# FFN output projection of a hybrid block: all 22 row tiles per span of 512, 256, 256 tokens instead of six groups of row tiles

## The chip, the cores and the metric

The kernel runs on one core of one Trainium2 chip. The metric is the device time of the program in microseconds (us); three executions of the kernel before took 2463.94, 2464.05 and 2467.35 us, and their median is what the changed kernel is compared with. In this text PE is the matrix engine (PEld its weight load), DVE the vector engine, ACT the scalar engine, POOL the GpSimd engine, SP the engine that issues nearly all DMAs (its rows are marked SPq; ACTq is ACT's own DMA queue).

## The reference

One layer of a streaming encoder: a mixer sub-layer (sparse attention beside a Mamba-2 mixer) and a SwiGLU sub-layer, both with a norm before and after. Only the end of the second one is touched:

```python
    h2 = rmsnorm(x, pre_norm_ffn) * (1.0 + scale_f) + shift_f
    u_gate, u_up = jnp.split(h2 @ w_ffn_in, 2, axis=-1)
    f = (jax.nn.silu(u_gate) * u_up) @ w_ffn_out
    x = x + gate_f * rmsnorm(f, post_norm_ffn)
```

There are 1024 tokens, `D_MODEL` is 1024 and `D_FF` 2816, all in float32. The matrix `a = silu(u_gate) * u_up` has 22 row tiles of 128 features (`FT` = 22); f has 8 row tiles of 128.

## The kernel before

Everything is held transposed: features on the 128 partitions, tokens along the row. Each float32 operand of a matmul is split into a high part (rounded to the matmul's `float32r`) and a low part (the rest), and each product is three matmuls: high x high, high x low, low x high. The high part is made by an ACT copy, the low part by a subtraction on DVE or POOL (`split_to`). Weights of one tile of f are read in pieces of up to four 128x128 blocks (256 KB).

`gate_up(t)` makes row tile t of `a` for both halves of 512 tokens and writes it to DRAM (`d_a`); the writes are `d_a<-g` (half 1) and `d_a<-p` or `d_a<-g` (half 0) on SP. The last call (t = 21) runs into the stage that is changed.

The FFN output projection then goes over six groups of 4, 4, 4, 4, 3 and 3 row tiles of `a` (`FFN_GROUPS`). For a group, both halves of `a` are read (`al`, nine buffers of the pool EV) and split (`ah`, `al`); for each of the 8 tiles of f the group's weights come through the stream `W` (four raw buffers, three for the high and three for the low part), and 12 (or 9) matmuls per half make a partial sum in PSUM (`pfo`). The first group's sums are copied to SBUF (`facc`) by ACT, those of the next four are added to it by DVE (line 1398).

The last group is different. Its weights are split beforehand into `foh`, `fol`, and it goes over three spans of tokens, `LAST` = 512, 256 and 256. For a span and each t, `sums` runs 9 matmuls (`pfl`), adds them to `facc` (DVE, line 1414), squares (ACT, line 1416) and sums the squares (DVE `sqm`, line 1418). `rstd` is the norm: matmuls of the squares with ones (line 260), one DVE operation (263) and a power on POOL (265). `rspread` spreads it with PE transposes (`prn`, line 271). `outputs` multiplies `facc` by the gate `gf` and the norm (DVE, 1429), adds the residual `x1l` (read on SP; added by POOL, in the last span by DVE for every second tile, line 1430) and writes `out`. The norm and outputs of a span are written between the sums of the next (after its tiles 2 and 4).

A list scheduler sets the order of each engine's instructions; in the last group PE keeps the order of the code (`in_order`). Each engine and each DMA queue runs its instructions strictly in that order, and a buffer is used again when its last reader is done.

Of the kernel before, what the change touches and what calls it, by code (L numbers as in the profile page):

```python
# [67 lines left out]
def build(tc, a, dbg=None, stop=99, slots=None):  # L68
    nc = tc.nc
    V, S, G, T, SP = nc.vector, nc.scalar, nc.gpsimd, nc.tensor, nc.sync  # L70
    ctx = ExitStack()
# [147 lines left out]
    def dense(outs, pcs, xs):  # L219


        for pi, ((hi, lo), k0, ks) in enumerate(pcs):
            for o, b, sl in outs:
                for i, k in enumerate(ks):
                    for wt, xi in ((hi, 0), (hi, 1), (lo, 0)):
                        T.matmul(o, wt[:, k0 + i, :], xs[k][xi][b][:, sl],  # L226
                                 start=pi == 0 and i == 0 and wt is hi and xi == 0,
                                 stop=pi == len(pcs) - 1 and i == len(ks) - 1 and wt is lo)
# [12 lines left out]
    def wpieces(ks, n=4):  # L241

        return [(W.next(), 0, ks[i:i + n]) for i in range(0, len(ks), n)]

    def split_to(src, hi, lo, lo_eng=None):
        S.activation(hi, src, AF.Copy)
        (lo_eng or V).tensor_tensor(lo, src, f(hi), op=OP.subtract)
# [20 lines left out]
    def rspread(r, nt=4):  # L268
        pt = bank("prn")
        for t in range(nt):  # L270
            T.transpose(pt[:, t * P:(t + 1) * P], r[:, t:t + 1].to_broadcast([P, P]), ident)
        return pt
# [1097 lines left out]
    for t in range(FT):  # L1370
        gate_up(t)

    facc = [R(f"facc{t}") for t in range(8)]
    f0 = 0
    NG = len(FFN_GROUPS)
    for gi, gn in enumerate(FFN_GROUPS):
        AH = [([None, None], [None, None]) for _ in range(gn)]
        for t in range(gn):
            for b in BS:
                r = EV("al")  # L1380
                SP.dma_start(r, d_a[f0 + t][:, half(b)])
                AH[t][0][b], AH[t][1][b] = split(Q if gi % 2 else H_, r, "a")
        ks = list(range(gn))

        def ffn_out(t):
            W.plan([(a["w_ffn_out"][t][:, f0:f0 + gn], gn)])
            return wpieces(ks)

        if gi < NG - 1:
            for t in range(8):  # L1390
                p = [bank("pfo") for b in BS]
                dense([(p[b], b, ALL) for b in BS], ffn_out(t), AH)
                for b in BS:
                    fv = facc[t][:, half(b)]
                    if gi == 0:
                        S.activation(fv, p[b], AF.Copy)
                    else:
                        V.tensor_tensor(fv, fv, p[b], op=OP.add)  # L1398
        else:
            fo = []  # L1400
            for t in range(8):
                raw = W.tile(0, F32)
                SP.dma_start(raw[:, :gn], a["w_ffn_out"][t][:, f0:f0 + gn])
                hi, lo = H_("foh", (P, gn, P), F32R), H_("fol", (P, gn, P), F32R)
                split_to(raw[:, :gn], hi, lo, lo_eng=G)
                fo.append((hi, lo))
            def sums(b, c0, cn):

                sacc = None
                for t in range(8):  # L1410
                    p = bank("pfl")[:, 0:cn]
                    dense([(p, b, slice(c0, c0 + cn))], [(fo[t], 0, ks)], AH)
                    fv = facc[t][:, 512 * b + c0:512 * b + c0 + cn]
                    V.tensor_tensor(fv, fv, p, op=OP.add)
                    sq = EV("sqm")[:, 0:cn]
                    S.activation(sq, fv, AF.Square)
                    if t:
                        V.tensor_tensor(sq, sq, sacc, op=OP.add)
                    sacc = sq
                    yield sacc  # L1420

            def outputs(b, c0, cn, r, end):
                cl = slice(512 * b + c0, 512 * b + c0 + cn)
                prf = rspread(r, cn // P)[:, 0:cn]
                for t in range(8):
# [3 lines left out]
                    V.scalar_tensor_tensor(fv, fv, gf[:, t:t + 1], prf, op0=OP.mult, op1=OP.mult)
                    (V if t % 2 and end else G).tensor_tensor(xr, xr, fv, op=OP.add)  # L1430
                    (S if t % 2 and end else SP).dma_start(a["out"][t][:, cl], xr)

            before = None
            with in_order(mybir.EngineType.PE):
                for span in LAST:
                    for t, sacc in enumerate(sums(*span)):
                        if before and t == 2:
                            before[3] = rstd([before[3]], D, nt=before[2] // P)
                        if before and t == 4:
                            outputs(*before, False)  # L1440
                    before = [*span, sacc]
                before[3] = rstd([sacc], D, nt=before[2] // P)
                outputs(*before, True)
        f0 += gn
# [76 lines left out]
```

## Time and profile before

| what | value |
|---|---|
| device time, three executions | 2463.94, 2464.05, 2467.35 us (median 2464.05) |
| the profiled execution, first to last instruction | 2459.8 us, mean granted clock of PE 0.988 |
| busy share: PE, PEld, DVE, ACT, POOL | 97%, 79%, 61%, 48%, 42% |
| changed stage, first matmul of `pfo` to the end | 2191.97 to 2459.8 us |
| DMA over the span | 341 MB, mean 139 GB/s |

A span is counted inside the program, from the first instruction to the last, so a device time is some 4 us more. Times in a timeline are microseconds from the start of the span. In a row of the timeline stand start, duration, engine, line, operation, output<-inputs, shape and count; what stands in brackets is the idle time before and who ended it. Matmuls overlap: one of 512 columns shows 0.39 us, but the next starts earlier, so its cost is the distance of two starts. In a row of groups, the numbers behind the bar are total busy us and mean ns of one, then the idle time before.

### The profile page before, as it was taken

What the parts mean: (1) busy time and instruction counts of PE and PEld (TensorE: products, weight loads), DVE (VectorE), ACT (ScalarE), POOL (GpSimd) and SP (SyncE); (2) the same over time, 40 slices, a digit from 0 to 9 for tenths busy, and PEclk for the clock granted to TensorE, in tenths of its full rate; (3) what the DMA queues carried; (4) which work ended last, traced back from release to release, by engine and by line L of the source; (5) the groups of instructions that cost most, each with busy time, mean ns of one, the idle gap of its engine ahead of it and who ended that gap; (6) DMA issues with size and microseconds to landing.
All of it is one profiled execution on the core that took longest, in us unless ns stands there. A gap on an engine that the chain in (4) does not pass through costs nothing. (4 is left out here: it accounts for less than half of the span.)

```text
span 2459.8 us, 34881 instructions
## 1 busy us (share of the span) xinstructions
PE 2383.1 (97%) x11946; PEld 1931.1 (79%) x11946; DVE 1496.3 (61%) x3050; ACT 1183.7 (48%) x2285; POOL 1022.3 (42%) x829
## 2 busy tenths in 40 slices
PE   7999999999999999999999999999999999999996
PEld 5788888888788887777776767888777888888886
DVE  4566775698745556765558666455476666552336
ACT  4446665567445545556566565544454222352211
POOL 2722112222234334553336335656676555432233
PEclk9999999999999999999999999999999999999998
DMA  7224122523212222223768775654465444253132
GB/s 268 99 77 130 65 73 78 155 87 103 86 67 92 102 99 91 93 84 123 223 215 260 228 246 172 231 186 161 168 208 171 160 145 163 99 190 113 48 99 90
DMA packets 212834, 341.25 MB, mean 139 GB/s; under 512 B 21249, under 2 KB 85425, under 8 KB 212657
## 3 DMA queue, kind: packets, MB, share of 16 engines
q1 hardware_dynamic: 211936, 338.45, 41.6%
q8 instruction: 94, 1.54, 0.3%
q14 instruction: 84, 0.68, 0.1%
q10 hardware_dynamic: 720, 0.58, 0.1%
HBM read 254.77 MB, written 87.32 MB: 139 GB/s over the span
## 5 line engine op out<-in xcount | busy, mean ns | idle before, releaser
L152 POOL TENSOR_TENSOR wlo<-wraw,whi 128x512 fp32r<-128x512 f32 (+1 forms) x282 | 380.7, 1351 | 769.4 <-ACT whi L151 698.5
L151 ACT ACTIVATE whi<-wraw 128x512 fp32r<-128x512 f32 (+1 forms) x282 | 175.4, 623 | 319.0 <-PE pfo L226 110.5
L1283 PE MATMUL p<-xh,wr 128*128 128x512 f32 x880 | 274.4, 391 | 3.8 <-DVE g L1333 3.6
L1283 PEld LDWEIGHTS p<-xh,wr 128*128 128x128 f32 x880 | 165.8, 188 | 39.1 <-DVE g L1333 4.0
L1277 POOL TENSOR_TENSOR wr<-a,wr 128x512 fp32r<-128x512 f32 x110 | 152.7, 1402 | 103.6 <-ACT wr L1276 70.6
L1283 PE MATMUL p<-xl,wr 128*128 128x512 f32 x440 | 171.8, 391 | 0.0
L778 ACT ACTIVATE lg<-lg,mx 128x256 f32<-128x256 f32 (+7 forms) x128 | 98.2, 769 | 74.7 <-DVE mx L775 73.5
L1276 ACT ACTIVATE wr<-a 128x512 fp32r<-128x512 f32 x110 | 67.7, 628 | 123.1 <-PE p L1283 98.0
L226 PE MATMUL pfo<-ah,wlo 128*128 128x512 f32 x304 | 118.1, 389 | 0.0
L226 PE MATMUL pfo<-al,whi 128*128 128x512 f32 x304 | 117.9, 389 | 0.0
L226 PE MATMUL pfo<-ah,whi 128*128 128x512 f32 x304 | 117.8, 389 | 0.0
L317 POOL TENSOR_TENSOR adaw<-adaw,cs 128x512 f32<-128x512 f32 x64 | 66.7, 1044 | 114.7 <-DMA adaw<-ada_w 109.4
L1398 DVE TENSOR_TENSOR facc<-facc,pfo 128x512 f32<-128x512 f32 x64 | 43.9, 686 | 112.0 <-PE pfo L226 112.0
L1283 PE MATMUL p<-h2h,wr 128*128 128x512 f32 x352 | 111.1, 393 | 0.0
L638 ACT ACTIVATE junk<-acc,cand__2203 128x1024 bf16<-128x1024 f32 (+2 forms) x96 | 86.2, 898 | 45.5 <-DVE cand__2203 L681 28.0
L226 PE MATMUL pos<-yw,whi 128*128 128x512 f32 x256 | 101.7, 397 | 3.6 <-DVE yw L1126 3.6
L226 PE MATMUL pos<-yh,whi 128*128 128x512 f32 x256 | 101.4, 396 | 1.7 <-ACT yh L1125 1.7
L226 PE MATMUL pos<-yh,wlo 128*128 128x512 f32 x256 | 101.5, 397 | 1.1 <-POOL wlo L152 1.1
L589 DVE SCALAR_TENSOR_TENSOR acc<-rel,widx,acc 128x384 f32<-128x384 f32 (+2 forms) x90 | 87.0, 986 | 24.9 <-ACT rel L584 24.7
L584 ACT ACTIVATE rel<-prel 128x512 f32<-128x512 f32 (+3 forms) x160 | 77.3, 524 | 48.4 <-PE prel L583 44.8
L1283 PEld LDWEIGHTS p<-xl,wr 128*128 128x128 f32 x440 | 83.0, 189 | 17.4
L799 PE MATMUL pt<-ident,lg 128*128 128x128 f32 x576 | 87.4, 277 | 7.1 <-ACT lg L778 6.6
(573 smaller groups left out, 6978.2 us busy)
## 6 DMA issues: line engine op xcount, KB each, us to landing
wraw<-w_in SPq DMA_DIRECT2D x130, 256.0 KB, 2.6
a<-w_ffn_in SPq DMA_DIRECT2D x124, 256.0 KB, 3.0
adaw<-ada_w SPq DMA_DIRECT2D x64, 256.0 KB, 2.7
al<-d_ac SPq DMA_DIRECT2D x32, 512.0 KB, 5.8
wraw<-w_o_ssd SPq DMA_DIRECT2D x64, 256.0 KB, 3.2
al<-d_a SPq DMA_DIRECT2D x44, 256.0 KB, 5.3
d_a<-g SPq DMA_DIRECT2D x40, 256.0 KB, 2.5
ada<-ada_p SPq DMA_DIRECT2D x16, 512.0 KB, 6.5
```

Of the source, the lines that this page charges most:

```text
L151: behind(S.activation(hi[:, :kt], raw[:, :kt], AF.Copy))
L152: behind(G.tensor_tensor(lo[:, :kt], raw[:, :kt], f(hi[:, :kt]), op=OP.subtract))
L226: T.matmul(o, wt[:, k0 + i, :], xs[k][xi][b][:, sl], start=pi == 0 and i == 0 and wt is hi and xi == 0, stop=pi == len(pcs) - 1 and i == l ...
L317: behind(G.tensor_tensor(t, t, cs[:, 4 * h:4 * h + 4, None].to_broadcast([P, 4, P]), op=OP.mult))
L584: S.activation(rel[:, 512 * b:512 * b + w_], pr[:, 0:w_], AF.Relu)
L589: V.scalar_tensor_tensor(acc[i][:, 0:n], rel[:, 0:n], ws, acc[i][:, 0:n], op0=OP.mult, op1=OP.add)
L638: S.activation(jk, y, AF.Sign, scale=-1.0, bias=a_, accum_out=o)
L778: S.activation(lg[:, 0:n], lg[:, 0:n], AF.Exp, scale=-1.0, bias=m, accum_out=mx[:, 3:4])
L799: T.transpose(ptv[:, hh, t, :], PR[hh, t][:, j * P:(j + 1) * P], ident)
L1276: S.activation(w[:, 0], src, AF.Copy)
L1277: G.tensor_tensor(w[:, 1], src, f(w[:, 0]), op=OP.subtract)
L1283: T.matmul(p, w[:, wi, i], X[x][i][xi], start=start and i == 0 and k == 0, stop=i == 3 and k == 2, skip_group_check=True)
```

## The change

The six groups and `facc` go. For each span of `LAST` all 22 row tiles of `a` are read and split at once (`a_load`), and for each tile t of f a single sum of 66 matmuls runs in one PSUM bank, with six weight pieces (`ffn_w`: k = 0-3, 4-7, ..., 20-21). The weights are read and split anew in each span: 48 pieces per span, 144 in all, where there were 48 loads. In the spans of 256 the low part of every second piece is made by DVE, otherwise by POOL. Four raw buffers remain; the high and low parts have five places. ACT squares the sum straight from PSUM and copies it, scaled with `gf`, to `fv`; `outputs` then multiplies by the norm only. The next span's `a` is loaded after tile 3 of the present span, a span's norm stands after tile 1 and its outputs after tile 2 of the next.

```diff
-    facc = [R(f"facc{t}") for t in range(8)]
-    for gi, gn in enumerate(FFN_GROUPS):
...
-        if gi < NG - 1:
-            for t in range(8):
-                p = [bank("pfo") for b in BS]
-                dense([(p[b], b, ALL) for b in BS], ffn_out(t), AH)
-                for b in BS:
-                    fv = facc[t][:, half(b)]
-                    if gi == 0:
-                        S.activation(fv, p[b], AF.Copy)
-                    else:
-                        V.tensor_tensor(fv, fv, p[b], op=OP.add)
...
-                    dense([(p, b, slice(c0, c0 + cn))], [(fo[t], 0, ks)], AH)
-                    fv = facc[t][:, 512 * b + c0:512 * b + c0 + cn]
-                    V.tensor_tensor(fv, fv, p, op=OP.add)
-                    sq = EV("sqm")[:, 0:cn]
-                    S.activation(sq, fv, AF.Square)
...
-                    xr = Q("x1l")[:, 0:cn]
-                    SP.dma_start(xr, d_x1[t][:, cl])
-                    fv = facc[t][:, cl]
-                    V.scalar_tensor_tensor(fv, fv, gf[:, t:t + 1], prf, op0=OP.mult, op1=OP.mult)
...
+    def a_load(s, b, c0, cn):
+        xs = []
+        for k in range(FT):
+            raw = EV("al")[:, 0:cn]
+            SP.dma_start(raw, d_a[k][:, 512 * b + c0:512 * b + c0 + cn])
+            hi, lo = a_tile(s, k, cn)
+            split_to(raw, hi, lo)
+            xs.append((hi, lo))
+        return xs
...
+    slots_hi = [("w1", n_slots["hi"])] * 3 + [("adaw", 2)] * 2
+    slots_lo = [("w2", n_slots["lo"])] * 3 + [("uh", 1), ("ul", 1)]
+    def ffn_w(t, k0, n, share):
+        i = len(pieces)
+        raw = w_tile(0, "fw")[:, 0:n]
...
+        SP.dma_start(raw, a["w_ffn_out"][t][:, k0:k0 + n])
+        split_to(raw, hi, lo, lo_eng=V if share and i % 2 else G)
...
+    def sums(s, b, c0, cn, fv):
+        xs, sacc = XS[s], None
+        for t in range(8):
+            p = bank("pfo")[:, 0:cn]
+            for k0 in range(0, FT, 4):
+                n = min(4, FT - k0)
+                w = ffn_w(t, k0, n, s > 0)
+                for k in range(k0, k0 + n):
+                    for i, (wi, xi) in enumerate(P3):
+                        T.matmul(p, w[wi][:, k - k0], xs[k][xi], start=k == 0 and i == 0, stop=k == FT - 1 and i == 2)
+            sq = EV("sqm")[:, 0:cn]
+            S.activation(sq, p, AF.Square)
+            S.activation(fv[t], p, AF.Copy, scale=gf[:, t:t + 1])
+            if t:
+                V.tensor_tensor(sq, sq, sacc, op=OP.add)
+            sacc = sq
+            yield sacc
...
+            xr = EV("x1l")[:, 0:cn]
+            SP.dma_start(xr, d_x1[t][:, cl])
+            V.tensor_tensor(fv[t], fv[t], prf, op=OP.mult)
+            (V if t % 2 and end else G).tensor_tensor(xr, xr, fv[t], op=OP.add)
+            (S if t % 2 and end else SP).dma_start(a["out"][t][:, cl], xr)
...
+        for s, (b, c0, cn) in enumerate(LAST):
+            fv = f_tiles(s, cn)
+            for t, sacc in enumerate(sums(s, b, c0, cn, fv)):
+                if t == 3 and s + 1 < len(LAST):
+                    XS.append(a_load(s + 1, *LAST[s + 1]))
+                if before and t == 1:
+                    before[4] = rstd([before[4]], D, nt=before[2] // P)
+                if before and t == 2:
+                    outputs(*before, False)
```

Up to the first weight load of this stage all engines run the same instructions in the same order as before. Three places in the new order matter below.

SP at the start of the stage (`al<-d_a` are reads of `a`, `wraw` and `fw` weight pieces, `d_a<-` the last writes of `gate_up`), before:

```order
L1349 DMA d_a<-g_20243 128x512
L150 DMA wraw<-w_ffn_out 128x512
L1356 DMA d_a<-p_20204 128x512
L1381 DMA al<-d_a 128x512 x13
L1349 DMA d_a<-g_20380 128x512
L1381 DMA al<-d_a 128x512 x4
L1356 DMA d_a<-p_20341 128x512
L1381 DMA al<-d_a 128x512 x7
```

and now:

```order
L1348 DMA d_a<-g_20243 128x512
L1417 DMA fw<-w_ffn_out 128x512
L1355 DMA d_a<-p_20204 128x512
L1395 DMA al<-d_a 128x512 x13
L1348 DMA d_a<-g_20380 128x512
L1395 DMA al<-d_a 128x512 x3
L1355 DMA d_a<-p_20341 128x512
L1395 DMA al<-d_a 128x512 x5
L1417 DMA fw<-w_ffn_out 128x512
L1395 DMA al<-d_a 128x512
```

The stream of reads is the same, but 22 of them are now what the first tile of f needs, where before 8 were.

POOL around the norm of the first span (`r` is the norm, `x1l` the residual add), before:

```order
L152 TENSOR_TENSOR wlo<-wraw,whi 128x384
L247 TENSOR_TENSOR fol<-wraw,foh 128x384 x3
L265 TENSOR_TENSOR r<-v,nhalf 128x4
L1430 TENSOR_TENSOR x1l<-x1l,facc_20454 128x512
L1430 TENSOR_TENSOR x1l<-x1l,facc_20455 128x512
```

and now:

```order
L246 TENSOR_TENSOR fwl<-fw,fwh 128x512 x9
L264 TENSOR_TENSOR r<-v,nhalf 128x4
L246 TENSOR_TENSOR fwl<-fw,fwh 128x512 x3
L1448 TENSOR_TENSOR x1l<-x1l,fv 128x512 x2
L246 TENSOR_TENSOR fwl<-fw,fwh 128x512
L1448 TENSOR_TENSOR x1l<-x1l,fv 128x512 x6
L246 TENSOR_TENSOR fwl<-fw,fwh 128x512 x20
```

Before, POOL had nothing left but adds; now the low parts of weight pieces stand behind them: counted from the first piece of the stage as 0, the single `fwl` is piece 72 and the one after the six adds is piece 74.

SP at the outputs of the second span, before (from here on SP only issued outputs and residual reads):

```order
L1403 DMA wraw<-w_ffn_out 128x384 x8
L1427 DMA x1l<-d_x_109 128x256 x6
L1431 DMA out<-x1l 128x512 x2
L1427 DMA x1l<-d_x_109 128x256
L1431 DMA out<-x1l 128x512
```

and now:

```order
L1446 DMA x1l<-d_x_109 128x256 x6
L1449 DMA out<-x1l 128x256 x2
L1446 DMA x1l<-d_x_109 128x256
L1449 DMA out<-x1l 128x256 x2
L1446 DMA x1l<-d_x_109 128x256
L1417 DMA fw<-w_ffn_out 128x512 x2
L1449 DMA out<-x1l 128x256
L1417 DMA fw<-w_ffn_out 128x512
```

Weight pieces (here 121 to 123) now stand behind `out` writes, each of which waits for a residual add.

More of the change, by code (lines that the diff above doesn't have):

```diff
@@ L1371, in build @@
         gate_up(t)
-    facc = [R(f"facc{t}") for t in range(8)]
-    f0 = 0
-    NG = len(FFN_GROUPS)
-    for gi, gn in enumerate(FFN_GROUPS):
-        AH = [([None, None], [None, None]) for _ in range(gn)]
-        for t in range(gn):
-            for b in BS:
[L1380 to L1387, printed above, removed]
-        if gi < NG - 1:
-            for t in range(8):
-                p = [bank("pfo") for b in BS]
-                dense([(p[b], b, ALL) for b in BS], ffn_out(t), AH)
-                for b in BS:
-                    fv = facc[t][:, half(b)]
-                    if gi == 0:
-                        S.activation(fv, p[b], AF.Copy)
-                    else:
-                        V.tensor_tensor(fv, fv, p[b], op=OP.add)
-        else:
[L1400 to L1411, printed above, removed]
-                    dense([(p, b, slice(c0, c0 + cn))], [(fo[t], 0, ks)], AH)
-                    fv = facc[t][:, 512 * b + c0:512 * b + c0 + cn]
-                    V.tensor_tensor(fv, fv, p, op=OP.add)
-                    sq = EV("sqm")[:, 0:cn]
[L1416 to L1425, printed above, removed]
-                    xr = Q("x1l")[:, 0:cn]
-                    SP.dma_start(xr, d_x1[t][:, cl])
-                    fv = facc[t][:, cl]
[L1429 to L1444, printed above, removed]
@@ new lines, in build, with a_tile @@
+    places = {0: [H_] * 16 + [Q] * 6, 1: [Q] * 14 + [R] * 8, 2: [H_] * 22}
+    half_r = []
+    def a_tile(s, k, cn):
+        where, w = places[s][k], F32R
+        if cn == 512:
+            return where("ah", dt=w), where("al", dt=w)
+        if where is not R:
+            t = where("a", (P, 2, 256), w)
+        elif half_r:
+            t = half_r.pop()
+        else:
+            pair = R("a", (P, 2, 2, 256), w)
+            half_r.append(pair[:, 1])
+            t = pair[:, 0]
+        return t[:, 0], t[:, 1]
@@ new lines, in a_load, with f_tiles @@
+    def a_load(s, b, c0, cn):
[7 more added lines that the diff above has]
+        return xs
+    def f_tiles(s, cn):
+        where, n = (R, 1024 // cn) if cn == 512 else (H_, 2)
+        ts = [where("fv", (P, n, cn)) for _ in range(8 // n)]
+        return [ts[t // n][:, t % n] for t in range(8)]
@@ new lines, in build @@
+    slots_hi = [("w1", n_slots["hi"])] * 3 + [("adaw", 2)] * 2
+    slots_lo = [("w2", n_slots["lo"])] * 3 + [("uh", 1), ("ul", 1)]
+    pieces = []
+    def ffn_w(t, k0, n, share):
+        i = len(pieces)
+        raw = w_tile(0, "fw")[:, 0:n]
+        hi, lo = (wp.tile([P, 4, P], F32R, name=nm, tag=tag, bufs=bufs)[:, 0:n]
+                  for nm, (tag, bufs) in (("fwh", slots_hi[i % 5]), ("fwl", slots_lo[i % 5])))
+        SP.dma_start(raw, a["w_ffn_out"][t][:, k0:k0 + n])
+        split_to(raw, hi, lo, lo_eng=V if share and i % 2 else G)
+        pieces.append((hi, lo))
+        return hi, lo
@@ new lines, in outputs @@
+    def outputs(b, c0, cn, fv, r, end):
+        cl = slice(512 * b + c0, 512 * b + c0 + cn)
+        prf = rspread(r, cn // P)[:, 0:cn]
+        for t in range(8):
+            xr = EV("x1l")[:, 0:cn]
[3 more added lines that the diff above has]
+            (S if t % 2 and end else SP).dma_start(a["out"][t][:, cl], xr)
+    before, XS = None, [a_load(0, *LAST[0])]
@@ new lines, in build @@
+    with in_order(mybir.EngineType.PE):
+        for s, (b, c0, cn) in enumerate(LAST):
[7 more added lines that the diff above has]
+                    outputs(*before, False)
+            before = [b, c0, cn, fv, sacc]
+        before[4] = rstd([sacc], D, nt=before[2] // P)
+        outputs(*before, True)
```

1 line of the change is left out of this document (removed).

## The prediction, made before the changed kernel ran

> **What bounds the kernel now.** I read the busy table first, then a table of stretches of the last 300 us, then PE's timeline there, then who made the gaps.
>
> ```profile
> span 2459.8 us, 34881 instructions
> PE 2383.1 (97%) x11946; PEld 1931.1 (79%) x11946; DVE 1496.3 (61%) x3050; ACT 1183.7 (48%) x2285; POOL 1022.3 (42%) x829
> ...
> 2240.00:2360.00 120.00, 120.00 (x531) 99.35 (x530) 36.08 (x52) 18.79 (x30) 28.44 (x23) 1.00 0.18 52
> ...
> 2417.00:2430.00 13.00, 11.91 (x97) 11.55 (x96) 10.31 (x21) 2.97 (x7) 5.48 (x5) 1.00 0.30 103
> 2430.00:2444.00 14.00, 10.00 (x69) 9.81 (x69) 11.22 (x25) 3.08 (x8) 9.07 (x10) 0.88 0.46 160
> 2444.00:2460.00 16.00, 1.89 (x8) 1.22 (x6) 9.32 (x21) 1.16 (x3) 7.19 (x10) 0.60 0.36 122
> ```
>
> The columns are length, busy us of PE, PEld, DVE, ACT, POOL, then PE's clock, the DMA share and GB/s. In the groups (2240 to 2360) PE never rests and the rest is idle more than two thirds of the time, with 52 GB/s of DMA. Only the two spans of 256 tokens (from 2417) and the tail lose PE time. So the stage is worth what PE's matmuls cost, plus these gaps.
>
> ```profile
> 2191.97 0.84 PE L226 MATMUL pfo<-ah,whi 128*128 128x512 f32 x3
> ...
> 2401.41 0.39 PE L226 MATMUL pfl<-ah,foh 128*128 128x512 f32 x1
> ...
> 2417.50 0.39 PE L226 MATMUL pfl<-ah,fol 128*128 128x512 f32 x1
> 2417.73 0.28 PE L226 MATMUL pfl<-ah,foh 128*128 128x256 f32 x1
> ...
> 2420.84 0.28 PE L226 MATMUL pfl<-ah,fol 128*128 128x256 f32 x1
> 2420.96 0.95 PE L260 MATMUL p<-ones,sqm 128*128 128x1 f32 x8
> 2421.78 0.36 PE L226 MATMUL pfl<-ah,foh 128*128 128x256 f32 x1
> ...
> 2424.01 0.60 PE L271 MATMUL prn<-ident,r 128*128 128x128 f32 x4
> 2424.36 0.36 PE L226 MATMUL pfl<-ah,foh 128*128 128x256 f32 x1
> ...
> 2430.21 0.36 PE L226 MATMUL pfl<-ah,foh 128*128 128x256 f32 x1 [1.30 <-DVE facc L1429]
> ...
> 2432.30 0.28 PE L226 MATMUL pfl<-ah,fol 128*128 128x256 f32 x1
> 2436.38 0.61 PE L260 MATMUL p<-ones,sqm 128*128 128x1 f32 x4 [3.79 <-DVE sqm L1418]
> 2436.84 0.39 PE L226 MATMUL pfl<-ah,foh 128*128 128x256 f32 x1
> ...
> 2440.23 0.39 PE L226 MATMUL pfl<-al,foh 128*128 128x256 f32 x1
> ...
> 2443.91 0.28 PE L226 MATMUL pfl<-ah,fol 128*128 128x256 f32 x1
> ```
>
> A 512-column matmul costs (2417.50 - 2401.41) / 71 = 0.2266 us, one of 256 columns (2420.84 - 2417.73) / 26 = 0.1196 us: two halves cost 0.0126 us more than one whole. After the wait of 3.79 us 16 matmuls took 3.39 us, 0.21 each: the clock was halved (0.88 in that stretch), which cost 1.5 us.
>
> **PE without waits.** Before, the stage has 984 matmuls of 512 and 144 of 256; after, 528 and 1056. From 2191.97, with the 12 matmuls of `gate_up` that stand in between (2.7): 528 x 0.2266 + 1055 x 0.1196 + 2.7 = 248.5, plus the norms inside the stream. Those of a 512 span cost 0.9 and 0.4 (2420.96 to 2421.78 and 2424.01 to 2424.36, and a slow first matmul each), of a 256 span half of it: 2.0 together. The last matmul would start 250.5 us after the first; in the trace it is 2443.91 - 2191.97 = 251.9. So the narrow matmuls cost 456 x 0.0126 = 5.7 us and the vanished gaps (1.3, 3.8, the halved clock, short ones) give back a little more: **-1.4**.
>
> **What is removed on other engines.** The 88 DVE adds into `facc` and 16 ACT copies lay beside a busy PE: nothing, except in the tail.
>
> ```profile
> 2444.58 0.88 DVE L1418 TENSOR_TENSOR sqm<-sqm 128x256 f32<-128x256 f32 x1
> ...
> 2446.04 2.35 DVE L1418 TENSOR_TENSOR sqm<-sqm 128x256 f32<-128x256 f32 x3
> 2448.45 1.01 PE L260 MATMUL p<-ones,sqm 128*128 128x1 f32 x4 [4.26 <-DVE sqm L1418]
> ...
> 2451.30 3.22 DVE L1429 SCALAR_TENSOR_TENSOR facc<-facc,gf,prn 128x256 f32<-128x256 f32 x8 [1.57 <-PE prn L271]
> ```
>
> **The tail.** DVE is behind here: PE's norm matmul starts 4.5 us after the last sum starts. With 66 matmuls (7.9 us) per tile DVE is not behind any more, and the chain is the matmul (0.28), one ACT square (0.42 for 256 columns, row below), one DVE add (0.43): about 1.2. That saves 3.3; PE at full clock saves some 0.4 of the 1.01; a multiply without `gf` perhaps 0.5 of the 3.22. **-4.0** (-3.3 to -4.5). What follows (adds, `out`) stays.
>
> **The start.** All 22 tiles are wanted within one row tile of f.
>
> ```profile
> 2195.19 1.89 DVE L247 TENSOR_TENSOR al<-al,ah 128x512 fp32r<-128x512 f32 x3
> ...
> 2206.79 1.99 DVE L247 TENSOR_TENSOR al<-al,ah 128x512 fp32r<-128x512 f32 x3 [1.17 <-ACT ah L246]
> 2209.61 3.94 DVE L247 TENSOR_TENSOR al<-al,ah 128x512 fp32r<-128x512 f32 x6 [0.83 <-ACT ah L246]
> ```
>
> The 10th split tile was ready at 2197.1, the 20th at 2208.8, the 22nd at 2210.9. PE now uses one per 0.68 us and wants the 22nd at 2209. The rate is set by the same buffers, with five ACT weight splits instead of five copies: **+1.5** (0 to 4).
>
> **What feeds PE now.** Per piece ACT and POOL or DVE work, in each span anew.
>
> ```profile
> L152 POOL TENSOR_TENSOR wlo<-wraw,whi 128x512 fp32r<-128x512 f32 x29 | 37.6, 1297 | 137.4 <-ACT whi L151 137.4
> L151 ACT ACTIVATE whi<-wraw 128x512 fp32r<-128x512 f32 x31 | 19.6, 632 | 103.9 <-PE pfo L226 93.0 <-issue 9.0 <-POOL wr L1277 1.8
> L1416 ACT ACTIVATE sqm<-facc 128x256 f32<-128x256 f32 x16 | 6.3, 418 | 20.9 <-DVE facc L1414 20.9
> ...
> 2425.53 10.51 POOL L1430 TENSOR_TENSOR x1l<-x1l,facc 128x512 f32<-128x512 f32 x8 [2.33 <-DVE facc L1429]
> ...
> 2432.08 1.43 DVE L1418 TENSOR_TENSOR sqm<-sqm 128x256 f32<-128x256 f32 x1
> ...
> 2439.88 0.43 DVE L1418 TENSOR_TENSOR sqm<-sqm 128x256 f32<-128x256 f32 x1 [0.48 <-ACT sqm L1416]
> ...
> wraw<-w_ffn_out SPq DMA_DIRECT2D x18, 256.0 KB, 2.6
> ...
> a<-w_ffn_in SPq DMA_DIRECT2D x56, 256.0 KB, 3.1
> ...
> x1l<-d_x SPq DMA_DIRECT2D x8, 256.0 KB, 5.1
> ...
> x1l<-d_x SPq DMA_DIRECT2D x9, 128.0 KB, 2.4
> ```
>
> A piece lasts PE 12 x 0.2266 = 2.72 us in the span of 512, and POOL's 1.30 is hidden. In the spans of 256 (span 2 and span 3 below) it lasts 1.435 us, a tile 7.9; POOL owes three pieces per tile (3.9 us), DVE three. On average enough; the place where it fails is the norm of the first span.
>
> **Span 2, POOL.** Let T be the start of its tile 3 (piece 66). PE wants piece 72 at T + 7.9 and piece 74 at T + 10.8. POOL has two adds, piece 72, six adds, then piece 74. The residual reads are issued near T (behind piece 72's read, which waits for a raw buffer) and land 2.6 (an idle queue) to 5.1 us later (the eight together). Two adds at 10.51 / 8 = 1.31, piece 72 at 1.30, six adds, piece 74 at 1.30: 13.1 us of work, done at T + 15.7 to T + 18.2, so PE waits 4.9 to 7.4. Nearest is eight reads together, but the first ones land earliest: I take **+6** (5 to 8, as DVE operations come in between). Such a wait is longer than the one that halved the clock: **+1.5** (0 to 3).
>
> **Span 2, queues.** In tiles 3 to 7 SP also carries the next `a`, and weight reads stand behind `out` writes that wait for those adds. Pieces and `a` are 5 x 1.44 + 2.9 MB, residuals and outputs 4.2 MB, in 39 us 366 GB/s, where the stage so far ran at 52. **+2** (0 to 6).
>
> **Span 3.** From the start of its tile 3, four adds of half width on POOL (some 0.75 each, half of 1.31 and a fixed part) end 5 to 7 us later, as the reads land after 2.4 to 5.1; only then the fourth `out` goes, and piece 121 behind it: read 2.6 to 3.1, split 0.63 on ACT and 0.7 to 1.4 on DVE (0.66 alone, 1.43 beside POOL), ready at 9.3 to 12.5, wanted at 9.3. **+2.5** (0 to 5).
>
> The weights' 96 more reads, DVE's and ACT's new splits outside these places are covered by the 7.9 or 15 us of PE per tile; without that cover each late piece would cost its 1.3.
>
> **Sum.** -1.4 - 4.0 + 6 + 1.5 + 2 + 2.5 + 1.5 = +8.1. The profiled execution's span is 2459.8; on it that gives 2467.9, and on the median of 2464.05, which holds the launch around it, 2472.
>
> **Rivals.** *Not slower: the adds do not hold PE.* The five places per part let the splits run ahead; if POOL's piece 74 is ready before T + 10.8, PE waits only at the start and for clock nothing: -5.4 + 1.5 + 0 to 2, 2460 to 2462. It decides at six adds of less than about 0.5 us, or reads that are issued well ahead of T. Against it: POOL's 1.31, back to back in the row, and its fixed order.
>
> *The weight stream itself bounds both narrow spans.* A raw buffer turns in read + 0.63 + 1.30, and four pieces last 5.74: it decides at reads of 3.8 us. Speaking against: 3.1 while `w_ffn_in` ran at 179 GB/s, near the 182 needed here; for: 5.1 in a burst. At 4.2 the turn is 6.13, and 88 full pieces / 4 x 0.4 = 9 us more than the sum: 2481; at 5.1, 1.29 x 22 = 28 more, 2500.
>
> *DVE and POOL exclude each other.* An add of two SBUF inputs took DVE 0.43 alone and 1.43 beside POOL's adds, while POOL's stayed at 1.31: here DVE pays, POOL hardly. If both paid fully, tiles 3 to 7 of span 2 need 30 us of POOL (15 pieces, 8 adds) and 20 of DVE (10 pieces at 3.94 / 6 = 0.66; 5 half pieces, 5 sums and 22 `a` splits at 0.43) in 39.5: 10.5 late instead of 6 + 2, and as much again of half that in span 3: 2475 to 2479. The Trainium skill ("SBUF — State Buffer", "Who interferes with whom") states this rule: a DVE instruction with two SBUF inputs and a GpSimd one that reads SBUF hold one port as a lock, and the later one blocks fully. This trace agrees for DVE (0.43 to 1.43), and not for POOL.
>
> **Chances.** The forecast (2465 to 2480) 0.55, not slower 0.13, weight stream 0.14, exclusion 0.18. The range 2460 to 2486 takes in the first, the last and the low end of the weight stream; what is left out is mostly above. 0.2% is 4.9 us, about what a measurement can tell from no change: the first rival's low end gives faster 0.05, its rest and the forecast's low part same 0.26, the rest slower 0.69.
>
> **What would show it.** Steps of 0.227 and 0.120 us in PE's stream right up to the waits; one PE wait of 5 to 8 us on POOL at the third piece of span 2's tile 4 and slower matmuls behind it; small waits at the first tile and in span 3's tile 4; the norm matmul of the tail about 1.2 us after the last sum. Waits in every tile of the narrow spans would be the weight stream. The forecast is wrong if that one wait is missing, or if narrow matmuls with ever new weights step above 0.120.

## The result, and the profile after

The changed kernel took 2480.43 us (median of four executions, 2478.97 to 2482.94) beside 2463.99 of the kernel before: a ratio of 1.0067, 95% interval 1.0052 to 1.0081, so it is slower, by 16.4 us. The prediction was slower, 2472 within 2460 to 2486. Direction and range hold; the number is 8.4 us too low, and the sections below look for these 8.4.

In the page, PE's busy time has grown by 13.5 us only. The table of stretches shows where the rest lies. The first four rows are the span of 512 tokens, span 2, span 3 and the tail (columns as before: length, busy us of PE, PEld, DVE, ACT, POOL, then PE's clock, DMA share, GB/s); the others are pieces of spans 2 and 3.

```profile
span 2477.8 us, 36315 instructions
PE 2396.6 (97%) x12402; PEld 1959.3 (79%) x12402; DVE 1494.6 (60%) x3032; ACT 1241.0 (50%) x2411; POOL 1086.9 (44%) x877
...
2193.77:2317.87 124.10, 123.11 (x542) 101.20 (x540) 34.04 (x51) 52.49 (x99) 54.62 (x45) 1.00 0.48 148
2317.87:2393.37 75.50, 68.16 (x542) 66.59 (x541) 40.40 (x62) 39.97 (x84) 42.71 (x32) 0.98 0.75 237
2393.37:2466.24 72.87, 68.37 (x536) 67.44 (x534) 32.10 (x40) 31.64 (x62) 37.84 (x32) 0.93 0.61 189
2466.24:2477.80 11.56, 1.31 (x9) 0.79 (x7) 5.15 (x14) 0.75 (x2) 3.48 (x5) 0.66 0.31 102
...
2352.00:2360.00 8.00, 2.91 (x18) 2.09 (x16) 5.18 (x4) 3.99 (x8) 8.00 (x7) 1.00 0.96 355
2360.00:2368.00 8.00, 7.91 (x53) 7.91 (x54) 5.14 (x10) 4.05 (x10) 2.77 (x3) 0.79 0.94 304
...
2432.00:2440.00 8.00, 6.83 (x33) 6.61 (x34) 2.98 (x4) 4.20 (x7) 4.29 (x4) 0.54 0.75 237
```

The stage lasts 2477.8 - 2193.77 = 284.0 us, where it lasted 267.8. It also began 1.8 us later, behind an identical program. That start lay between 2188.9 and 2198.4 in the profiled executions of this study, so below I compare lengths of the stage. (A device time is 1.8 us over its span in every execution on record with both, not some 4 as was said ahead of the prediction.) Without any wait each span of 256 would take about 64 (528 x 0.1196 = 63.1 and the norm's own matmuls, some more of them in span 2); span 2 lost 11 us and span 3 lost 9. The loss is in two places, both where the residual of the span before is handled. In the first POOL is busy all the time, PE 2.91 us of 8, and the DMA share is 0.96; in the second the clock fell to 0.54. PE's timeline names the waits (in brackets: idle time, and who ended it):

```profile
2342.86 0.48 PE L1432 MATMUL pfo<-a,fwh 128*128 128x256 f32 x2
...
2353.34 0.50 PE L1432 MATMUL pfo<-a,fwh 128*128 128x256 f32 x2 [0.89 <-ACT fwh L245]
2354.64 0.39 PE L1432 MATMUL pfo<-a,fwl 128*128 128x256 f32 x1 [0.80 <-DVE fwl L246]
2356.54 0.50 PE L1432 MATMUL pfo<-a,fwh 128*128 128x256 f32 x2 [0.44 <-ACT fwh L245]
2360.09 0.39 PE L1432 MATMUL pfo<-a,fwl 128*128 128x256 f32 x1 [3.05 <-POOL fwl L246]
...
2418.26 0.48 PE L1432 MATMUL pfo<-a,fwh 128*128 128x256 f32 x2
...
2428.87 0.41 PE L1432 MATMUL pfo<-a,fwl 128*128 128x256 f32 x1 [2.22 <-POOL fwl L246]
2433.17 0.80 PE L1432 MATMUL pfo<-a,fwh 128*128 128x256 f32 x2 [1.97 <-ACT fwh L245]
...
2467.45 0.61 PE L259 MATMUL p<-ones,sqm 128*128 128x1 f32 x4 [0.93 <-DVE sqm L1437]
```

2342.86 and 2418.26 are the starts of tile 3 in spans 2 and 3. The waits at 2353.34 and 2356.54 are for pieces 73 and 74 (numbered from 0 at the stage's first), the one at 2360.09 for piece 74's low part on POOL, those at 2428.87 and 2433.17 for pieces 120 and 121. What stood behind them, on POOL, ACT and SP:

```profile
2348.75 1.57 POOL L246 TENSOR_TENSOR fwl<-fw,fwh 128x512 fp32r<-128x512 f32 x1
2350.28 8.08 POOL L1448 TENSOR_TENSOR x1l<-x1l,fv 128x512 f32<-128x512 f32 x6
...
2352.65 0.63 ACT L245 ACTIVATE fwh<-fw 128x512 fp32r<-128x512 f32 x1 [6.14 <-DMA fw<-w_ffn_out]
...
2342.89 3.27 SPq L1446 DMA_DIRECT2D x1l<-d_x  x7
2346.26 0.38 SPq L1417 DMA_DIRECT2D fw<-w_ffn_out  x1
...
2420.30 2.80 SPq L1446 DMA_DIRECT2D x1l<-d_x  x6
2424.05 1.22 SPq L1449 DMA_DIRECT2D out<-x1l  x2
2425.32 0.42 SPq L1446 DMA_DIRECT2D x1l<-d_x  x1
2426.94 1.01 SPq L1449 DMA_DIRECT2D out<-x1l  x2
2428.04 0.39 SPq L1446 DMA_DIRECT2D x1l<-d_x  x1
2428.52 0.87 SPq L1417 DMA_DIRECT2D fw<-w_ffn_out  x2
...
2432.48 1.30 ACT L245 ACTIVATE fwh<-fw 128x512 fp32r<-128x512 f32 x2 [4.20 <-DMA fw<-w_ffn_out]
...
fw<-w_ffn_out SPq DMA_DIRECT2D x18, 256.0 KB, 4.2
```

POOL's six adds are the predicted block. Beside it stands a second delay: piece 73's read was issued at 2346.26 behind seven residual reads, ACT had it at 2352.65, 6.4 us later, and piece 121's read was issued 10.3 us after its tile 3 began and ACT had it 4.0 us later. Before it SP issued no weight read from 2420.3 to 2428.5. The last row is the median from issue to landing of the 18 full weight reads between 2344 and 2385: 4.2 us.

### The profile page after: what moved, and what is told of

It reads as the page before. It is cut to its first block, busy times and chain, and to the rows that moved or that the text cites. A ratio compares the mean times of both kernels' runs of the same rounds, so it can differ in the third digit from the quotient of the medians.

```text
span 2477.8 us, 36315 instructions
## 1 busy us (share of the span) xinstructions
PE 2396.6 (97%) x12402; PEld 1959.3 (79%) x12402; DVE 1494.6 (60%) x3032; ACT 1241.0 (50%) x2411; POOL 1086.9 (44%) x877
## 4 chain that ended last, share of the span: by engine, by line
PE 72%; DVE 10%; DMA 8%; ACT 3%; issue 3%; POOL 3%; SPq 1%; POOLq 0%; ACTq 0%; DVEq 0%
PE pw L225 17%; PE p L1282 13%; PE pfo L1432 6%; PE pos L225 5%; PE plg L765 4%; PE pw L235 3%; PE poa L235 3%; PE po L814 3%; PE pot L225 3%; PE pt L798 3%; PE prel L582 3%; PE puq L225 2%; DVE junk L635 2%; DMA fw<-w_ffn_out 2%; ACT junk L637 1%
## 5 line engine op out<-in xcount | busy, mean ns | idle before, releaser
L151 POOL TENSOR_TENSOR wlo<-wraw,whi 128x512 fp32r<-128x512 f32 x242 | 331.2, 1370 | 611.3 <-ACT whi L150 553.7
L150 ACT ACTIVATE whi<-wraw 128x512 fp32r<-128x512 f32 x242 | 151.0, 626 | 191.4 <-issue 46.6
L246 POOL TENSOR_TENSOR fwl<-fw,fwh 128x512 fp32r<-128x512 f32 x96 | 123.4, 1288 | 142.4 <-ACT fwh L245 132.4
L245 ACT ACTIVATE fwh<-fw 128x512 fp32r<-128x512 f32 x144 | 85.4, 595 | 128.0 <-PE pfo L1432 76.4
L1432 PE MATMUL pfo<-a,fwh 128*128 128x256 f32 x704 | 132.8, 291 | 3.7 <-ACT fwh L245 3.7
L1432 PEld LDWEIGHTS pfo<-a,fwh 128*128 128x128 f32 x704 | 113.6, 198 | 4.8 <-ACT fwh L245 4.8
L1432 PE MATMUL pfo<-a,fwl 128*128 128x256 f32 x352 | 102.6, 291 | 8.1 <-POOL fwl L246 7.3
L1282 PEld LDWEIGHTS p<-xl,wr 128*128 128x128 f32 x440 | 82.8, 188 | 17.2
```

Of the source, the lines that this page charges most:

```text
L150: behind(S.activation(hi[:, :kt], raw[:, :kt], AF.Copy))
L151: behind(G.tensor_tensor(lo[:, :kt], raw[:, :kt], f(hi[:, :kt]), op=OP.subtract))
L1282: T.matmul(p, w[:, wi, i], X[x][i][xi], start=start and i == 0 and k == 0, stop=i == 3 and k == 2, skip_group_check=True)
L1432: T.matmul(p, w[wi][:, k - k0], xs[k][xi], start=k == 0 and i == 0, stop=k == FT - 1 and i == 2)
```

## The experiments

Two accounts were to be told apart at first: *theory A*, the residual's reads and adds make the losses, and *rival B*, the weight stream (reads and splits) bounds the narrow spans. Rival C blames the next `a`, rival D the exclusion of DVE and POOL. All edits are to the changed kernel. Times are medians; lengths of the stage and of spans 2 and 3 are from one profiled execution each. Single executions of one kernel differ by up to 15 us (e9: 2463.5 to 2478.1), so a difference of 1 or 2 us between two lengths shows little.

| run | median, us | before, us | ratio (95%) | stage | span 2 | span 3 |
|---|---|---|---|---|---|---|
| changed kernel | 2480.4 | 2464.0 | 1.0067 (1.0052 to 1.0081) | 284.0 | 75.5 | 72.9 |
| e1 no residual | 2467.2 | 2465.0 | 1.0012 (1.0001 to 1.0022) | 273.0 | 71.4 | 65.8 |
| e2 adds on DVE | 2481.7 | 2465.0 | 1.0068 (1.0056 to 1.0080) | 284.3 | 76.2 | 72.5 |
| e3 `out` by POOL | 2487.8 | 2465.0 | 1.0089 (1.0076 to 1.0102) | 290.7 | 82.9 | 71.7 |
| e4 residual early | 2483.5 | 2465.0 | 1.0067 (1.0055 to 1.0079) | 281.8 | 81.2 | 65.4 |
| e5 next `a` paced | 2480.9 | 2467.0 | 1.0053 (1.0040 to 1.0066) | 284.6 | 75.8 | 71.3 |
| e6 = e4 + e5 | 2476.4 | 2467.0 | 1.0046 (1.0029 to 1.0062) | 278.9 | 77.6 | 65.4 |
| e7 all paced | 2481.5 | 2467.0 | 1.0058 (1.0042 to 1.0074) | 283.5 | 80.2 | 67.2 |
| e8 no residual, paced | 2473.2 | 2467.0 | 1.0023 (1.0012 to 1.0034) | 273.1 | 71.7 | 65.9 |
| e9 more raw places | 2470.6 | 2466.0 | 1.0019 (1.0005 to 1.0032) | 272.1 | 71.3 | 65.1 |
| e10 = e9, paced | 2468.8 | 2466.0 | 1.0010 (0.9999 to 1.0021) | 274.0 | 74.5 | 63.9 |
| e11 = e9, adds split | 2466.2 | 2464.7 | 1.0008 (0.9996 to 1.0019) | 270.1 | 68.7 | 64.3 |
| e12 = e9 + e2 | 2462.2 | 2464.7 | 0.9987 (0.9975 to 1.0000) | 266.0 | 67.2 | 63.9 |

### e1: no residual in the first two spans

```diff
+            V.tensor_tensor(fv[t], fv[t], prf, op=OP.mult)
+            if not end:
+                SP.dma_start(a["out"][t][:, cl], fv[t])
+                continue
             xr = EV("x1l")[:, 0:cn]
             SP.dma_start(xr, d_x1[t][:, cl])
```

> Left out: the residual reads and adds of the outputs of the first two spans; their `out` writes stay and send the normed f itself. Theory A (the residual's reads and adds make the losses: eight reads of 256 KB in one burst ahead of weight reads, and eight adds on POOL ahead of weight low parts): the 11.5 us lost in span 2 and the 8.2 us in span 3 fall to 2 us or less each, 2462 to 2466. Rival B (the weight stream itself bounds the narrow spans; 96 weight reads and the `out` writes are all still there): at most half of it comes back, 2470 to 2476. Rival C (the 22 reads and splits of the next `a`, which start just behind, make the loss of span 2): span 2 keeps 6 us or more and only span 3 gains, 2470 to 2474.

2467.2, a little above what theory A gives and clearly below B and C; the stage is 11 us shorter. Span 3 keeps 2 us of its 9. Span 2 keeps 7 of 11, though, far more than the 2 expected: something else loses time there. In the stage PE still waits 1.9 us on ACT's high parts and 2.5 us on POOL's low parts, though POOL has no adds any more, and ACT waits eleven times for a weight read in span 2, 11.2 us in all. So reads are late there without the residual, too; this run could not say behind what.

### e2: the adds on DVE

```diff
-            (V if t % 2 and end else G).tensor_tensor(xr, xr, fv[t], op=OP.add)
+            (V if t % 2 or not end else G).tensor_tensor(xr, xr, fv[t], op=OP.add)
```

> The 16 residual adds of the first two spans on DVE in place of POOL; SP's reads and writes stay. If POOL's place in line is the whole cause, its waits of 3.1, 0.9, 0.9 and 2.2 us go and the clock with them: 2468 to 2471, unless DVE's own low parts come late in turn. If late reads are the larger part (Theory A's other half), the waits on ACT's high parts stay or grow, since DVE's eight adds of 0.7 to 0.9 us now stand ahead of every second low part: 2475 to 2480. If DVE and POOL exclude each other, DVE's low parts and adds last no longer than 0.9 us here, against 1.2 to 1.7 us beside POOL's adds, and it gains at least 8 us.

Nothing gained: 2481.7, just above the second case. PE's waits (us in total, times, longest) moved from POOL to ACT, as that case had it; here are e2's:

```profile
PE pfo L1432 <- ACT fwh L245: 6.7, 5, 1.9
PE pfo L1432 <- POOL fwl L246: 3.9, 5, 0.9
```

ACT itself waited 6.57 us for a weight read at the first place. So the six adds were not the only thing late at their place: with them gone, the reads of the same pieces hold PE nearly as long.

### e3: `out` issued by POOL

```diff
-            (S if t % 2 and end else SP).dma_start(a["out"][t][:, cl], xr)
+            (S if t % 2 and end else SP if end else G).dma_start(a["out"][t][:, cl], xr)
```

> The 16 `out` writes of the first two spans are issued by POOL, behind its own adds, in place of SP: no weight read stands behind an `out` write any more, and SP does not wait for POOL. If that queue is what makes reads late, the waits on ACT's high parts (0.9, 0.4, 0.4, 2.0 us) and part of the halved clock go: 2473 to 2476. If the reads are late because of the burst of residual reads itself, those waits stay and POOL's issues lengthen its waits: 2480 to 2486.

Slower, as the second case said, and 1.8 us above its range. The next rows are e3's POOL timeline, then its DMA issues between 2347 and 2366 (count, KB each, median us to landing): an issue costs POOL some 0.56 us or more of its own time, and the weight reads, with no `out` ahead of them on SP, still took 4.6.

```profile
2348.19 0.76 POOL L1449 DMA_DIRECT2D out<-x1l  x1
...
2351.43 0.56 POOL L1449 DMA_DIRECT2D out<-x1l  x1
...
fw<-w_ffn_out SPq DMA_DIRECT2D x5, 256.0 KB, 4.6
```

The Trainium skill ("DMA: Bandwidth & Descriptors", "Issuing engines are not separate DMA queues") says that transfers begun by several engines share the same DMA engines, and that another issuer saves only issue time. This run agrees.

### e4: the residual read early

```diff
-            xr = EV("x1l")[:, 0:cn]
+            xr = (EV if end else Q)("x1l")[:, 0:cn]
```

> The residual tiles of the first two spans lie in `Q`, where 12 places are free at that time, in place of `EV`. Their reads are then issued some 18 weight pieces earlier, away from the place; adds stay on POOL, four ahead of a low part in place of two and six. Theory A: the burst and the waits on ACT's high parts go, POOL's four adds still hold a low part by some 1 to 3 us in span 2 and 0 to 1 in span 3: 2465 to 2470. If POOL's adds alone are the cause: span 2 still waits 3 us or more on POOL with a halved clock behind it, 2473 to 2478. If the weight stream is the cause: no change, 2478 to 2482.

Span 3 is cured (65.4), span 2 is worse (81.2). With places of EV free, the scheduler put the reads of the next `a` ahead of piece 77. SP's rows, and what PE then waited for:

```profile
2353.34 0.33 SPq L1417 DMA_DIRECT2D fw<-w_ffn_out  x1
2353.73 2.88 SPq L1395 DMA_DIRECT2D al<-d_a  x3
...
2361.57 7.69 SPq L1395 DMA_DIRECT2D al<-d_a  x14
2369.32 1.85 SPq L1417 DMA_DIRECT2D fw<-w_ffn_out  x4
...
2373.17 0.80 PE L1432 MATMUL pfo<-a,fwh 128*128 128x256 f32 x2 [5.86 <-ACT fwh L245]
```

For 16 us no weight read was issued. None of the three cases foresaw this, and 2483.5 lies above all of them: it is not the residual as such that counts but whatever stands ahead of a weight read.

### e5, e6 and e8: the next `a` paced

A step behind each weight piece loads one row tile of the next `a`, in place of all 22 at once (e5; in span 1 too); e6 adds e4's edit, e8 e1's.

```diff
-                if t == 3 and s + 1 < len(LAST):
-                    XS.append(a_load(s + 1, *LAST[s + 1]))
...
                 w = ffn_w(t, k0, n, s > 0)
+                step(6 * t + k0 // 4)
...
+        if ahead and 18 <= j and (j - 18) * 22 // 28 > len(ahead[1]) - 1 and len(ahead[1]) < FT:
+            next(ahead[0])
```

> The 22 reads and splits of the third span's `a` are asked for one per weight piece from tile 3 of span 2 on, in place of all at once; the residual stays as it is. If the next `a` is the smaller part (e1 gave back 13 us without touching it), span 2 gains 1 to 4 us at its tiles 5 to 7 and span 3's loss of 8 us stays: 2476 to 2480. If the next `a` is the main part of span 2's loss, 2471 to 2475.

> e4 and e5 together: residual reads early (tiles in `Q`), the third span's `a` paced. Theory A, as e2 to e4 amended it (what counts is what stands ahead of a weight read on SP, whichever transfer it is, and POOL's block of adds comes on top): the 16 us without a weight read that e4 showed behind its `a` reads are gone, span 3 loses 2 us or less as in e4, and in span 2 only POOL's five adds in a row hold a low part, 3 to 6 us with the clock: 2466 to 2471. If the burst only changes its place again, 2476 to 2484.

> Left out: the residual reads and adds of the first two spans, as in e1; and the third span's `a` is paced as in e5. If the 6 us that e1 still lost in span 2 come from the next `a`, they go: 2460 to 2463. If they come from the eight `out` writes that stand together ahead of weight reads on SP, 2464 to 2468.

e5 gained nothing in span 2 (75.8), and e8 nothing over e1 in either span. e5's 2480.9 lies just above and e8's 2473.2 well above both of its cases; in their round the kernel before took 2467.0, some 3 us more than the cases were reckoned from. e6 missed theory A's case too (2476.4 where 2466 to 2471 was expected, at the edge of its second case): the 16 us without a read are gone, but span 2 still loses 13, with 3.0 us of waiting at once on the low part of piece 72, behind POOL's adds. Where `a` stands in the order is not the remaining cause.

### e7: everything paced

Residual reads one per four pieces (`Q`), adds one per three, each `out` three pieces later, the next `a` one per piece, and SP, POOL, ACT and DVE held to that order (`chain` makes an instruction follow the one chained before it on its engine).

```diff
+        if j in READ:
+            xr = Q("x1l")[:, 0:cn]
+            chain(SP.dma_start(xr, d_x1[len(late)][:, cl]))
+            late.append(xr)
+        if j in ADD:
+            t = ADD.index(j)
+            V.tensor_tensor(fv[t], fv[t], prn[0], op=OP.mult)
+            chain(G.tensor_tensor(late[t], late[t], fv[t], op=OP.add))
+        if j - 3 in ADD:
+            t = ADD.index(j - 3)
+            chain(SP.dma_start(a["out"][t][:, cl], late[t]))
...
+    READ, ADD = range(3, 48, 4)[:8], range(18, 48, 3)[:8]
```

> Same work, other order: in spans 2 and 3 the residual reads (tiles in `Q`) are one per four pieces, the adds one per three pieces on POOL, each `out` write three pieces behind its add, the next `a` one per piece, and SP, POOL, ACT and DVE are held to that order for reads, splits, adds and writes. Theory A: no PE wait over 0.6 us in the two spans, losses of 0 to 3 us together; with the tail's gain the kernel takes 2458 to 2464, so it is as fast as before or a little faster. Rival B (the weight stream bounds the narrow spans): waits spread over all tiles, 2470 or more. Rival D (DVE and POOL exclude each other): the same adds beside the same splits, so the loss stays at 6 us or more: 2468 to 2474.

Theory A as I had it expected no wait over 0.6 us, and the stage is as long as before the edit; the waits came in 18 pieces, most of them over tiles 3 to 7 of span 2, as rival B expects:

```profile
PE pfo L1450 <- POOL fwl L246: 4.4, 8, 0.9
PE pfo L1450 <- DVE fwl L246: 4.0, 6, 2.3
PE pfo L1450 <- ACT fwh L245: 2.1, 4, 1.2
```

But this does not refute theory A, for the edit made a hold-up of its own (e7's SP, then DVE):

```profile
2333.58 0.42 SPq L1407 DMA_DIRECT2D al<-d_a  x1
2342.21 0.34 SPq L1475 DMA_DIRECT2D out<-x1l  x1
...
2339.32 4.27 DVE L1471 TENSOR_TENSOR fv<-fv,prn 128x512 f32<-128x512 f32 x7
```

From 2334.0 to 2342.2 SP issued nothing: in the fixed order the first `out` write stands ahead of piece 70's read, and it waited for its add on POOL. The multiplies by the norm, which `chain` does not hold, were scheduled seven in a row on DVE, ahead of piece 67's low part; that is PE's wait of 2.3 us. What pacing alone is worth stays open.

I formed A' next: while the residual, `out` and the next `a` move, a weight read takes about 4 us (medians at this place: 4.2 in the changed kernel, 4.1 in e6, 4.0 here, though 3.0 in e4, where the reads stand on both sides of the burst); the turn of a raw buffer (read, 0.63 on ACT, 1.3 on POOL) is then over the 5.74 us that four pieces last, and reads cannot run ahead of the adds' block.

### e9: more raw places

```diff
-        raw = w_tile(0, "fw")[:, 0:n]
+        raw = (Q("fw", (P, 4, P)) if share and i % 2 else w_tile(0, "fw"))[:, 0:n]
```

> Every second weight piece of spans 2 and 3 is read into one of 12 free places of `Q` in place of the four raw buffers; nothing else is written differently. SP then issues weight reads up to 12 pieces ahead, so those of the place stand ahead of the residual's reads and writes. Theory A', after e7 (a read takes 4 to 7 us whenever residual, `out` and next `a` move too, wherever they are put, and four raw buffers hold less than that): ACT's waits on weight reads go, POOL's adds (two, four, one, one between low parts) still hold PE: 5 us or less lost in span 2, 3 or less in span 3, 2466 to 2471. If the order on POOL and the slowing of DVE beside POOL are the cause: 9 us or more in span 2, 2474 to 2481.

The stage fell by 11.9 us to 272.1, with the same work on each engine, and the time lies in the expected 2466 to 2471. All of PE's waits for weights outside the first tile of the stage are one kind (first row); the largest is the third row. The POOL row shows what it waited for, the last row the reads from 2341 to 2382.

```profile
PE pfo L1432 <- POOL fwl L246: 5.4, 3, 4.3
...
2339.77 0.48 PE L1432 MATMUL pfo<-a,fwh 128*128 128x256 f32 x2
...
2355.98 0.58 PE L1432 MATMUL pfo<-a,fwl 128*128 128x256 f32 x1 [4.28 <-POOL fwl L246]
...
2348.46 6.24 POOL L1448 TENSOR_TENSOR x1l<-x1l,fv 128x512 f32<-128x512 f32 x4
...
fw<-w_ffn_out SPq DMA_DIRECT2D x23, 256.0 KB, 4.5
```

The reads are no faster than in the changed kernel (4.5 us, 4.2 there). They are issued sooner (piece 73's 16 us before the start of tile 3, at 2339.77, where it was 3.4 us after it), and no wait on ACT is left. What is left is mainly the predicted wait, on piece 74 behind POOL's adds, 4.3 us and its slower clock; one of 1.0 us in span 3 is like it. One thing beside the reads changed with the edit: the scheduler put four adds ahead of piece 74's low part where there were six, so a part of the 4.2 us that span 2 gained may come from there. Span 3, which gained 7.8, has four adds ahead of piece 120's low part in both kernels.

### e10: more raw places, paced

The edits of e9 and e7 together, with `chain` on POOL only:

```diff
+            if i.engine not in (mybir.EngineType.Pool,):
+                continue
             if i.engine in chained:
```

> e9's raw places, and the residual reads, adds and next `a` spread as in e7, but only POOL held to an order (its low parts and adds). Theory A': neither late reads nor a block of adds are left, 0 to 4 us lost in spans 2 and 3 together, 2459 to 2465. If DVE beside POOL is what e7 still lost (its waits of 4.0 us on DVE's low parts): those waits stay at 3 us or more, 2466 to 2471. If neither, as e7: 2474 to 2482.

2468.8, within what the second case allowed. PE waited 5.6 us on DVE low parts, and this is why (e10's PE, then DVE):

```profile
2357.95 0.58 PE L1452 MATMUL pfo<-a,fwl 128*128 128x256 f32 x1 [3.86 <-DVE fwl L246]
...
2351.56 5.74 DVE L246 TENSOR_TENSOR a<-al,a 128x256 fp32r<-128x256 f32 x4
```

A subtraction of 128x256 takes DVE 0.41 us alone and 1.44 here, while POOL adds and splits without a pause. Rival D is real where both work at once, with DVE paying.

### e11 and e12: more raw places, adds moved

e11 gives DVE every second add on top of e9's edit, e12 all of them (e2's edit on e9).

```diff
-            (V if t % 2 and end else G).tensor_tensor(xr, xr, fv[t], op=OP.add)
+            (V if t % 2 else G).tensor_tensor(xr, xr, fv[t], op=OP.add)
```

> e9, with every second residual add of the first two spans on DVE in place of POOL (on POOL stand one, two and one adds between low parts, on DVE two, one and one). e9 lost 6.8 us in span 2, all of it in one wait of 4.3 us on POOL behind four adds and the halved clock after it, and 2.5 in span 3. If POOL's block is what is left, both go to 2 us or less each, and the kernel takes 2462 to 2467, the same as before within the bound. If DVE then pays what POOL saves (each of its adds waits for the end of a POOL operation, 1.4 us in place of 0.7), there is a wait of 2 us or more on a DVE low part: 2467 to 2472.

> e9, with all 16 residual adds of the first two spans on DVE (e2 with more raw places). e2 showed 6.7 us of waits on ACT and 3.9 on POOL; if those were late reads, none on ACT is left, and POOL, which has only low parts, makes none over 0.5 us. DVE has four, three and one adds between its low parts: at 0.7 us each it is in time and the kernel takes 2461 to 2466; at 1.4 us each (DVE waiting for POOL) PE waits 2 to 4 us on a DVE low part and for its clock, 2466 to 2472.

e11's 2466.2 lies in the first case, and yet its one wait in spans 2 and 3, 2.3 us, is on a DVE low part, as the second had it. e12 is the fastest kernel of the study: 2462.2, ratio to before 0.9987 (0.9975 to 1.0000). Its time lies in the first case, its wait of 2.3 us in the second, and the four adds in a row took 1.17 us each (4.67 / 4), between the two. It beats the changed kernel by far; against the kernel before it is 2.5 us ahead, but the interval reaches 1.0000, so it is not shown to be faster. Its rows: PE's waits, DVE and POOL at the place, and the reads there.

```profile
PE pfo L1432 <- DVE fwl L246: 2.3, 1, 2.3
...
2344.71 4.67 DVE L1448 TENSOR_TENSOR x1l<-x1l,fv 128x512 f32<-128x512 f32 x4
...
2353.25 0.41 DVE L1437 TENSOR_TENSOR sqm<-sqm 128x256 f32<-128x256 f32 x1
2353.59 1.78 DVE L246 TENSOR_TENSOR fwl<-fw,fwh 128x512 fp32r<-128x512 f32 x1
...
2352.12 2.70 POOL L246 TENSOR_TENSOR fwl<-fw,fwh 128x512 fp32r<-128x512 f32 x1 [3.88 <-DMA out<-x1l]
...
fw<-w_ffn_out SPq DMA_DIRECT2D x24, 256.0 KB, 5.0
```

The changed kernel, e2, e9 and e12 are the four corners of one table. By stage lengths, moving the adds alone makes it 0.3 us longer, more raw places alone 11.9 shorter, both 18.0 shorter. The medians, each less that of the kernel before in its own round, agree: +16.4, +16.7, +4.6 and -2.5. So POOL's block costs some 6 once the reads are early, and nothing to be seen while they are late: the two delays lie at one place and hide each other.

## Why the prediction was right, and where it was not

**"PE without waits" (-1.4) was right.** The steps are 0.227 and 0.120 us up to the waits. Span 3 without a wait (e12) is 63.9 us; the working gives 63.0 and the norm's 0.7.

**"The tail" (-4.0) was right.** Last sum to the end: 11.56 us, before 2459.8 - 2443.91 = 15.9, so -4.3. The norm's matmul comes 1.2 us after the last sum, as worked out.

**"The start" (+1.5) was right.** There are two waits of 0.5 us on DVE's `al`; the steps that hold them are 0.91 and 0.94 us long in place of 0.227, 1.4 us more together.

**"Span 2, POOL" (+6, and +1.5 for the clock) was right in place and cause, and in when piece 74 is ready, but not in the size of the wait.** Piece 74 was to be ready at T + 15.7 to T + 18.2; it was at 2360.09 - 2342.86 = T + 17.2, in e9 at T + 16.2. The single wait is 3.05 and not the 5 to 8 that were to show it, mainly because 2.1 us had just been lost on pieces 73 and 74's reads; with these early (e9) it is 4.28. The clock fell to 0.79 for 8 us behind it, 1.7 us.

**"Span 2, queues" (+2) was somewhat small.** Span 2 took 75.5 us, 11 over a clean one, where the terms had 9.5. e9, whose waits on reads are gone, takes 71.3: the reads cost up to 4.2 on top of POOL's block (whose order changed a little with e9), twice the term.

**"Span 3" (+2.5) is the step that failed.** It measured 72.9 - 63.9 = 9.0, and these 6.5 us are most of the 8.1 by which the stage was longer than predicted. The mechanism was the stated one, SP's order, but three sizes in it were wrong. The fourth `out` was put 5 to 7 us after tile 3's start, and piece 121's read right behind it; the read went out at 10.3, since the residual reads began 2.0 us after that start and the last two of them stood among the `out` writes ahead of it. It took 3.9 us to land, where I took 2.6 to 3.1 from a quiet stretch. And piece 120's low part stood behind the same four adds on POOL, a wait of 2.2 us that I had left out. With one of 0.3 in tile 0 these waits are 4.5 us; the other 4.5 are mostly the clock behind them, 0.82 and then 0.54 over 16 us, which I had priced for span 2 only. Where the residual is read long before (e4), span 3 takes 65.4.

The profiled span was 9.9 us over the predicted 2467.9: 8.1 by the stage, 1.8 by its later start. The way from 9.9 to 8.4 is that a device time is 1.8 us over its span here, and by that the profiled execution of before lay 2.5 us below the median, that of after 0.9.

Over both spans the forecast gave POOL's block and its clock 7.5 us and SP's order 4.5; e9 and e12 show some 6 and up to 12. The place and the direction were right, but the larger cause was taken for the smaller.

**Of the rivals**, "not slower" fell with the first wait. "The weight stream bounds both narrow spans" was wrong as put: away from the two places, with reads of 2.8 to 3.1 us, a wait of 0.3 us is all. Its condition, reads above 3.8 us, was met at the first place, though (4.2 in the median), and by four reads at the second (pieces 121 to 124, 3.9 to 4.4; the median from 2420 to 2445 is 2.8). In span 3 the reads were late more than slow. By e9 and e12 late reads cost more than POOL's block, up to 11.9 us of the stage beside 6.1. My error was to keep the two as alternatives. "DVE and POOL exclude each other" was not what made most of the 16 us, for e9 leaves every operation on its engine and gives back 11.9; where more is piled onto both (e10) it costs PE 5.6 us.

## What to carry to other kernels

When a stream is refilled through a few buffers, work out the turn of a buffer with the transfer time of the busiest stretch it crosses, not of the quiet one; if it is longer than those buffers last, reads cannot run ahead (in span 2 here 4.2 + 0.63 + 1.30 = 6.1 us beside 5.74). Count, too, what stands ahead of a read in its queue: in span 3 it was mainly this that made reads late. More places help against both: twelve made the stage 11.9 us shorter, while the six moves and reorderings tried here, e2 to e7, made it between 5.1 shorter and 6.7 longer (e7 with a hold-up of its own). Two delays at one place hide each other, so take both away before calling either harmless. A wait of 2 us is priced with the slower clock that may follow it.

## What the runs showed of the hardware

In these rows DVE and POOL hold each other up in both directions, and it looks as if who came first goes on. In e10 DVE's 0.41 us became 1.44 beside POOL's back-to-back work. In e12 it is the other way round: POOL's low part began at 2352.12 and took 2.70 us, where it takes 1.30 alone, while DVE ran several operations at full speed until 2353.59; DVE's next one then took 1.78. The Trainium skill ("SBUF — State Buffer", "Who interferes with whom") says just this: the issue order decides who blocks. The prediction's remark that the trace does not agree for POOL holds for the rows shown there only.

A weight read of 256 KB took 2.8 to 3.1 us from issue to landing where the changed kernel moved 138 to 211 GB/s (2300 to 2342 and 2385 to 2445), and 4.2 to 5.0 where the core moved 294 to 321 (changed kernel, e9, e12). After waits of about 2 us in a row PE's granted clock fell to 0.54 over 8 us (2432 to 2440). A single wait does not settle it: after e12's of 2.3 us the clock stayed at 1.00 (2346 to 2362), after e10's of 1.8 us (at 2380) it was 0.83 over 10 us. What decides between the two is not shown here.
